# An RWKV layer's work issued in one order written out by hand, in place of a scheduler's order

## The chip, the cores and the metric

The kernel runs on one core of a Trainium2 chip (core 0). The metric is the device time of one execution in microseconds (us). Of the kernel before there are three timed runs, and one further execution was taken by the hardware profiler. The engines are called as in the profile: PE is the matrix engine, PEld its weight loads, DVE the vector engine, ACT the scalar engine, POOL the GpSimd engine, and SP the queue from which all DMA transfers of this kernel are issued.

## The reference, cut to what matters

A stream x of 256 positions by 2048 channels passes an RWKV-7 layer with its MLP, a shared key and value projection, an attention layer with a second MLP, and a last norm. The change touches the first mixing layer only. What it computes:

```python
h = rms_norm(x, mix_norm[0]); prev = h shifted by one position
xs = h + (prev - h) * x_mix                  # six mixes: r, k, v, w, a, g
r, k, v = xs[r] @ w_rkv[0], xs[k] @ w_rkv[1], xs[v] @ w_rkv[2]
decay = exp(-exp(-softplus(-(w0 + tanh(xs[w] @ w1) @ w2)) - 0.5))
a = sigmoid(a0 + (xs[a] @ a1) @ a2);  g = sigmoid(xs[g] @ g1) @ g2
kk = normalised(k * k_k);  k = k * (1 + (a - 1) * k_a)
# per head, S is 64 x 64, frame by frame:
S = S * decay_t + (S @ -kk_t) (kk_t * a_t)^T + v_t k_t^T;   y_t = S @ r_t
y = group_norm(y) * lnx_w + lnx_b + sum(r * k * r_k) * v
x = x + (y * g) @ w_o
```

All weights and all data are float32.

## The kernel before, in words

The 256 positions stand in the free dimension, the 2048 channels in 16 groups of 128 partitions (KT = 16). A weight tile of 512 KB is loaded by `load_split` (L191): SP issues the load to a buffer `wr` (4 buffers), ACT casts it to `wh` (L203), and DVE writes the rest `wl = wr - wh` (L205). Each is a float32r operand, so that a product is made of three matmuls: `wh` by the high part of the data, `wh` by the low part, and `wl` by the high part (`mm3`, L210 to L213). `wh` and `wl` have 5 buffers each.

The layer is cut into streams, each a Python generator that yields between its steps: `h` makes the normalised stream and its differences, `mk`, `mr` and `mv` the mixes for k, r and v, `lw`, `la` and `lg` the small projections of decay, a and gate, `gk`, `gr`, `gv` (four each) the three big projections, `gate` the gate's second product, `prep0` to `prep7` what a unit of four heads needs ahead of its recurrence, `inv0` to `inv7` the inverse of a 64 x 64 triangle per chunk and head, `rec0` to `rec7` the recurrence in four chunks of 64 frames, and `wo0` to `wo3` the first 12 of 16 contraction steps of the output projection. The last four steps of `wo` follow as plain calls of `gemm_group`, and then the MLP begins, whose first matmul is the first that writes a tile `mmw`.

In `rec_steps` (L777) a chunk is a chain: four matmuls of `halves` (L869, tile `zyus`) give zp, DVE copies it to `zt` (L179), eight matmuls follow (L883, L887), ACT copies two halves into `Tt` (L177, "ua" and "ub"), eight more matmuls (L869) give the next state, and DVE adds them to `sw` into the next chunk's `Tt` (L897). POOL has made `sw` from the state before (L182). The inverse is a like chain of 64 x 64 matmuls (L693, tiles i0 to i5), with ACT's copies X and Y (L177) and DVE's product t1 (L731) between. These matmuls use a quarter of the array (tile 64 x 64) or half (128 x 64); those of the projections use all of it (128 x 128).

The order in which all this stands is made twice. `play` (L299) sorts the steps of all streams by the due times in PLAN_A and PLAN_B, and calls them in this order. What the steps issue is then put in order once more, engine by engine, by the scheduler of the language's tile layer, instruction by instruction, from priorities and its own estimate of durations. In part B `share` makes every 10th cast go to DVE (L201) and every 5th subtraction go to POOL (L205).

Of the kernel before, what the change touches and what calls it, by code (L numbers as in the profile page):

```python
# [14 lines left out]
ALU = mybir.AluOpType  # L15
# [38 lines left out]
def shape_constants():  # L54
# [13 lines left out]
    for s in range(6):  # L68
# [5 lines left out]
        if s == 0:  # L74
# [18 lines left out]
SHARE_A = {"h": 0, "l": 0}  # L93
SHARE_B = {"h": 10, "l": 5}
PLAN_A = {
# [6 lines left out]
}  # L102
PLAN_B = {
# [6 lines left out]
}  # L110
AFTER = {"gate": ["lg"], "mv": [f"gk{g}" for g in range(4)], "mr": [],
         "wo2": ["rec5"], "wo3": ["rec5"], "wo0": ["wo2", "wo3"], "wo1": ["wo2", "wo3"]}
AFTER.update({f"prep{u}": [f"gk{u // 2}", "lw", "la"] for u in range(8)})
AFTER.update({f"inv{u}": [f"prep{u}"] for u in range(8)})
AFTER.update({f"rec{u}": [f"inv{u}", "gr0", "gr1", "gr2", "gr3", f"gv{u // 2}", "gate"] for u in range(8)})
# [3 lines left out]
def trunk_kernel(ctx: ExitStack, tc: tile.TileContext, xin, vecs, bfv, c32, c16, w_rkv, w1, w2, a1, a2, g1, g2,  # L119
                 w_o, w_kvf, fox_q, fox_o, w_up, w_down, out):  # L120
    nc = tc.nc
    mm = nc.tensor.matmul
    act = nc.scalar.activation
    V = nc.vector
    G = nc.gpsimd
    dma = nc.sync.dma_start
    ldma = nc.sync.dma_start
    sdma = nc.sync.dma_start
    nc.scalar.preload_act_table_set("natural_log_exp_and_others")

# [44 lines left out]
    def cp(n, o, i):  # L175
        if ENG[n] == "S":
            nc.scalar.copy(o, i)  # L177
        else:
            (V if ENG[n] == "V" else G).tensor_copy(o, i)  # L179
# [11 lines left out]
    share = {"n": 0, "h": 0, "l": 0}  # L191

    def load_split(src, p, nk, n, per=1, wraw=wraw, wsp=wsp):
# [3 lines left out]
        for k in range(0, nk, per):  # L197
            h = wsp.tile([p, per, n], F32R, tag="wh", name="wh")
            c = share["n"] = share["n"] + 1
            if share["h"] and c % share["h"] == 0:  # L200
                V.tensor_copy(h, raw[:, k:k + per, :])  # L201
            else:
                nc.scalar.copy(h, raw[:, k:k + per, :])  # L203
            lo = wsp.tile([p, per, n], F32R, tag="wl", name="wl")
            (G if share["l"] and c % share["l"] == 0 else V).tensor_tensor(  # L205
                lo, raw[:, k:k + per, :], h.bitcast(F32), op=ALU.subtract)
            hl += [(h[:, i, :], lo[:, i, :]) for i in range(per)]
# [73 lines left out]
    def gemm_wide(w, col, x, name, pool, wpools, evac):  # L281

        ps = wide_sums(w, col, x, wpools)
        for b in range(2):
            t = pool.tile([P, 2, T], F32, tag=name, name=name, bufs=3)
            for j in range(2):
                nc.scalar.copy(t[:, j, :], ps[2 * b + j][:, T:2 * T])
# [7 lines left out]
    def play(plan, streams, finished):  # L295

        order = sorted((b + (e - b) * (j + 0.5) / (streams[n][1] + 1), i, n)
                       for i, (n, (b, e)) in enumerate(plan.items()) for j in range(streams[n][1] + 1))
        for _, _, n in order:  # L299
            if n not in finished:  # L300
                assert all(m in finished for m in AFTER.get(n, ())), n
                if next(streams[n][0], finished) is finished:
                    finished.add(n)
        assert all(n in finished for n in plan)
# [61 lines left out]
    def split(src, oh, ol, gp=False):  # L366
        nc.scalar.copy(oh, src)
# [3 lines left out]
    def mlp(layer, norm, pool, wpools, a, b, final):  # L371
# [29 lines left out]
        def finish(g):  # L401

            for j in range(2):
                kp = 2 * g + j
                tp = side("ytp").rearrange("p (k t) -> p k t", k=2)
                for kk in range(2):
                    for i in range(2):
                        n = (2 * kp + kk) * P
                        nc.tensor.transpose(tp[:, kk, i * P:(i + 1) * P], y[:, i, n:n + P], C("ident"))
# [4 lines left out]
        for c in range(FF // D):  # L414
            for g in range(4):
# [10 lines left out]
                if c == 0 and g == 3:  # L426
                    rps = side("rc")
                    for i in range(2):
                        nc.tensor.transpose(rps[:, i * P:(i + 1) * P], r2[:, i * P:(i + 1) * P], C("ident"))
# [53 lines left out]
    G.memset(hT[:, :, 0:1], 0.0)  # L483


# [3 lines left out]
    warm = side("warm")  # L489
    for i in range(12):  # L490
        mm(warm[:, 0:P], ones, ones, start=True, stop=True)
    ps = side("hps")[:, 0:T]
    for i, (k0, k1) in enumerate(XG):
        sq = hT[:, k0:k1, 1:]
        if i % 2 == 0:
            act(sq, xT[:, k0:k1, :], AF.Square)
        else:
            V.tensor_tensor(sq, xT[:, k0:k1, :], xT[:, k0:k1, :], op=ALU.mult)
# [716 lines left out]
```

## Time and profile before

| what | before |
|---|---|
| timed runs | 2467.97, 2468.21 and 2472.01 us; median 2468.21 us |
| the profiled execution, span from first to last instruction | 2470.1 us |
| PE, busy | 2426.3 us, 98% of the span |
| PEld, DVE, ACT, POOL, busy | 2085.5, 1510.2, 1237.9 and 241.2 us |
| first matmul of the MLP (tile mmw) | 641.1 us after the span's start |

The span of the profiled execution is 1.9 us above the median of the runs. A matmul of the profile is pipelined and its end is modelled, so that PE counts as busy from one matmul's start over the next one's: how far PE is from its best shows in the distance from one start to the next, not in its busy share. "PEclk" is the clock that PE was granted. A row of the timeline has the start, the time from the first start to the last end of the instructions merged in it, engine, line, tiles and shapes, and in brackets how long the engine had been idle and what ended that. "issue" means that nothing which the profile shows was waited for.

### The profile page before, as it was taken

What the parts mean: (1) busy time and instruction counts of PE and PEld (TensorE: products, weight loads), DVE (VectorE), ACT (ScalarE), POOL (GpSimd) and SP (SyncE); (2) the same over time, 40 slices, a digit from 0 to 9 for tenths busy, and PEclk for the clock granted to TensorE, in tenths of its full rate; (3) what the DMA queues carried; (4) which work ended last, traced back from release to release, by engine and by line L of the source; (5) the groups of instructions that cost most, each with busy time, mean ns of one, the idle gap of its engine ahead of it and who ended that gap; (6) DMA issues with size and microseconds to landing.
All of it is one profiled execution on the core that took longest, in us unless ns stands there. A gap on an engine that the chain in (4) does not pass through costs nothing.

```text
span 2470.1 us, 45757 instructions
## 1 busy us (share of the span) xinstructions
PE 2426.3 (98%) x18336; PEld 2085.5 (84%) x18336; DVE 1510.2 (61%) x2199; ACT 1237.9 (50%) x1971; POOL 241.2 (10%) x241
## 2 busy tenths in 40 slices
PE   8999999999999999999999999999999999999998
PEld 6899877689888888888888888888888888888886
DVE  8986575665854455554567565777654555555554
ACT  3766454454654453443455544565554543443543
POOL 2000122221310010000011000011010000000001
PEclk9999999999999999999999999999999999999999
DMA  5777765564756666666655656545656666656653
GB/s 165 229 248 247 260 212 174 183 181 154 229 182 196 194 185 194 194 188 192 192 181 178 191 178 195 173 154 178 202 182 196 188 188 195 191 188 196 190 185 125
DMA packets 276565, 472.56 MB, mean 191 GB/s; under 512 B 23280, under 2 KB 70656, under 8 KB 276352
## 3 DMA queue, kind: packets, MB, share of 16 engines
q1 hardware_dynamic: 276352, 469.64, 61.4%
q8 instruction: 143, 2.34, 0.4%
q14 instruction: 70, 0.57, 0.1%
HBM read 445.44 MB, written 24.13 MB: 190 GB/s over the span
## 4 chain that ended last, share of the span: by engine, by line
PE 91%; DVE 4%; issue 2%; DMA 2%; ACT 1%; POOL 0%; SPq 0%; POOLq 0%; DVEq 0%; ACTq 0%
PE mmw L253 21%; PE mmw L257 11%; PE mmd L391 9%; PE mmd L390 9%; PE mmd L389 9%; PE mmn L271 5%; PE mm L211 3%; PE mm L212 3%; PE mm L213 3%; PE mmn L275 2%; PE i L693 1%; PE mmv L767 1%; PE mmv L1047 1%; PE mmv L1046 1%; PE zyus L869 1%
## 5 line engine op out<-in xcount | busy, mean ns | idle before, releaser
L205 DVE TENSOR_TENSOR wl<-wr,wh 128x1024 fp32r<-128x1024 f32 (+1 forms) x1001 | 963.8, 974 | 774.6 <-ACT wh L203 683.5
L203 ACT CAST wh<-wr 128x512 fp32r<-128x512 f32 (+1 forms) x1012 | 841.0, 837 | 976.6 <-PE mmd L390 344.3
L253 PE MATMUL mmw<-opB,wh 128*128 128x512 f32 x1280 | 321.1, 392 | 0.0
L253 PEld LDWEIGHTS mmw<-opB,wh 128*128 128x128 f32 x1280 | 230.3, 189 | 41.8 <-ACT nln L351 0.3
L253 PE MATMUL mmw<-opA,wh 128*128 128x512 f32 x1024 | 256.6, 392 | 0.0
L253 PEld LDWEIGHTS mmw<-opA,wh 128*128 128x128 f32 x1024 | 184.3, 189 | 33.4 <-ACT nln L351 0.3
L389 PE MATMUL mmd<-wh,opA 128*128 128x512 f32 x512 | 199.6, 390 | 0.0
L389 PE MATMUL mmd<-wh,opB 128*128 128x512 f32 x512 | 199.6, 390 | 0.0
L391 PE MATMUL mmd<-wl,opA 128*128 128x512 f32 x512 | 199.2, 389 | 0.0
L390 PE MATMUL mmd<-wh,opB 128*128 128x512 f32 x512 | 199.2, 389 | 0.0
L391 PE MATMUL mmd<-wl,opB 128*128 128x512 f32 x512 | 199.2, 389 | 0.0
L390 PE MATMUL mmd<-wh,opA 128*128 128x512 f32 x512 | 199.2, 389 | 0.0
L419 POOL TENSOR_TENSOR ms<-mt 128x512 f32<-128x512 f32 x64 | 78.6, 1241 | 1158.0 <-ACT mt L417 1158.0
L257 PEld LDWEIGHTS mmw<-opB,wl 128*128 128x128 f32 x1280 | 174.5, 190 | 14.9 <-DVE wl L205 2.6
L257 PE MATMUL mmw<-opB,wl 128*128 128x256 f32 x1280 | 178.7, 282 | 1.8 <-DVE wl L205 1.8
L211 PE MATMUL mm<-opA,wh 128*128 128x256 f32 x512 | 150.5, 294 | 0.0
L257 PEld LDWEIGHTS mmw<-opA,wl 128*128 128x128 f32 x1024 | 139.7, 190 | 10.0
L213 PE MATMUL mm<-opA,wl 128*128 128x256 f32 x512 | 145.2, 284 | 0.8 <-issue 0.8
L212 PE MATMUL mm<-opA,wh 128*128 128x256 f32 x512 | 145.5, 284 | 0.0
L257 PE MATMUL mmw<-opA,wl 128*128 128x256 f32 x1024 | 142.8, 282 | 0.0
L391 PEld LDWEIGHTS mmd<-wl,opA 128*128 128x128 f32 x512 | 96.1, 188 | 20.0
L391 PEld LDWEIGHTS mmd<-wl,opB 128*128 128x128 f32 x512 | 96.1, 188 | 20.0
(293 smaller groups left out, 3818.5 us busy)
## 6 DMA issues: line engine op xcount, KB each, us to landing
wr<-in_mlp_w_up_dram SPq DMA_DIRECT2D x256, 512.0 KB, 3.8
wr<-in_mlp_w_down_dram SPq DMA_DIRECT2D x256, 512.0 KB, 4.0
wr<-in_w_rkv_dram SPq DMA_DIRECT2D x96, 512.0 KB, 4.8
wr<-in_w_kvf_dram SPq DMA_DIRECT2D x64, 512.0 KB, 3.7
wr<-in_w_o_dram SPq DMA_DIRECT2D x32, 512.0 KB, 4.2
wr<-in_fox_w_q_dram SPq DMA_DIRECT2D x32, 512.0 KB, 3.6
wr<-in_fox_w_o_dram SPq DMA_DIRECT2D x32, 512.0 KB, 3.6
wr<-in_g_dram SPq DMA_DIRECT2D x8, 512.0 KB, 4.5
```

The source lines that it names most:

```text
L203: nc.scalar.copy(h, raw[:, k:k + per, :])
L205: (G if share["l"] and c % share["l"] == 0 else V).tensor_tensor(lo, raw[:, k:k + per, :], h.bitcast(F32), op=ALU.subtract)
L211: mm(ps, wh, xh, start=first and bank_first, stop=False, skip_group_check=True)
L212: mm(ps, wh, xl, start=False, stop=False, skip_group_check=True)
L213: mm(ps, wl, xh, start=False, stop=last, skip_group_check=True)
L253: mm(ps[m], h[:, m * P:(m + 1) * P], x[:, k].rearrange("p h t -> p (h t)"), start=k == 0, stop=False, skip_group_check=True)
L257: mm(ps[m][:, 0:T], lo[:, m * P:(m + 1) * P], x[:, k, 0, :], start=False, stop=k == KT - 1, skip_group_check=True)
L271: mm(ps[m], hl[i][0][:, m * P:(m + 1) * P], x[:, k0 + i].rearrange("p h t -> p (h t)"), start=k0 + i == 0, stop=False, skip_group_check=True)
L389: mm(ps[i], b[:, k, 0, t], h, start=k == 0, stop=False)
L390: mm(ps[i], b[:, k, 1, t], h, start=False, stop=False)
L391: mm(ps[i], b[:, k, 0, t], lo, start=False, stop=k == KT - 1)
L419: G.tensor_tensor(s, t, t, op=ALU.mult)
```

## The change: what it does

A thin wrapper stands around each engine (`Tap`): while a `Tape` records, a call is not issued but noted, with the letter of its engine (P for PE, S for ACT, V for DVE, G for POOL, Q for SP) and the step it belongs to. All streams of part A, with the norm at the start as a stream of its own (`first`), are recorded, then those of part B. `record` cuts each stream into pieces: every instruction of ACT, DVE, POOL and SP is a piece, and for PE all matmuls of one step that follow each other. `replay` issues the pieces as two written tables say (2531 pieces, counted in them), and inside `tc.manual_schedule()` this order is the program order of every engine. What follows the layer is put behind its last instruction of each engine (`tc.issue_after`). The due times, `play` and `share` go, so all casts are ACT's and all subtractions DVE's. From the first matmul of the MLP on, the order of all five engines is as before. All instructions of the layer then come from one line (L251) in the changed kernel; L245 is all that is issued outside of the recording.

```diff
-SHARE_A = {"h": 0, "l": 0}
-SHARE_B = {"h": 10, "l": 5}
-PLAN_A = {
-    "mr": (2.914, 3.432), "gk2": (2.618, 3.513), "prep5": (4.992, 5.379), "gk3": (3.79, 4.651),
...
+ORDER_A = """
+firstG firstP lwQ*2 gk0Q firstS gk0Q prep0Q*2 firstP firstV*2 firstS firstP firstG firstV firstP firstV firstP
...
+ORDER_B = """
...
+rec7V wo1V rec7P wo3S wo3V wo1Q wo1S wo3Q*2 rec7S wo1P wo1V rec7S rec7V wo1P wo1S rec7V wo1V rec7S wo1P rec7V wo1S
...
+class Tape:
...
+    def record(self, gen):
+
+        self.ops, self.step = [], 0
+        for _ in gen:
+            self.step += 1
+        ops, self.ops = self.ops, None
+        return ops
...
+        def call(*a, **k):
+            if self._t.ops is None:
+                return f(*a, **k)
+            self._t.ops.append((self._l, self._t.step, f, a, k))
+        return call
...
-            c = share["n"] = share["n"] + 1
-            if share["h"] and c % share["h"] == 0:
-                V.tensor_copy(h, raw[:, k:k + per, :])
-            else:
-                nc.scalar.copy(h, raw[:, k:k + per, :])
+            S.copy(h, raw[:, k:k + per, :])
             lo = wsp.tile([p, per, n], F32R, tag="wl", name="wl")
-            (G if share["l"] and c % share["l"] == 0 else V).tensor_tensor(
-                lo, raw[:, k:k + per, :], h.bitcast(F32), op=ALU.subtract)
+            V.tensor_tensor(lo, raw[:, k:k + per, :], h.bitcast(F32), op=ALU.subtract)
...
+    def record(names):
+        for n in names:
+            last = None
+            for op in tape.record(streams[n]):
+                if op[0] != "P" or op[:2] != last:
+                    rec.setdefault(n + op[0], deque()).append([])
+                rec[n + op[0]][-1].append(op)
+                last = op[:2]
...
+    def replay(order):
+        with tc.manual_schedule():
+            for t in order.split():
+                n, _, c = t.partition("*")
+                for _ in range(int(c or 1)):
+                    for op in rec[n].popleft():
+                        last[op[0]] = emit(n[:-1], op)
...
+        for ins in last.values():
+            behind.enter_context(tc.issue_after(ins.ins))
```

Three places show how instructions move. The first is PE at the very start. Before, behind the norm's matmuls (`hps`), stand those of the first big projection (`mm`, whose data is `opB`):

```order
L491 MATMUL warm<-ones 128x128 x12
L502 MATMUL hps<-hT,ones 128x256 x10
L211 MATMUL mm<-opB,wh 128x256 x2
L212 MATMUL mm<-opB,wh 128x256
L213 MATMUL mm<-opB,wl 128x256
```

In the changed kernel the same place reads:

```order
L251 MATMUL warm<-ones 128x128 x12
L251 MATMUL hps<-hT,ones 128x256 x10
L251 MATMUL lps<-xs,wr 96x256 x8
L251 MATMUL mm<-opB,wh 128x256 x2
L251 MATMUL mm<-opB,wl 128x256
```

Eight matmuls of the decay's small projection (`lps`) have moved ahead of the first big one; they read a mix `xs` as it is, while `opB` is cast and subtracted from it first.

The second place is PE at the third chunk of unit 3 (`zyus_6987` before, `zyus_5315` now; `Tt_6548` and `Tt_5294` are that unit's state). Before, the four matmuls of the chunk's first step and the big ones of `gv` (`mmv`) stand in each other:

```order
L769 MATMUL mmv_7792<-wl_7801,opB_77 128x512
L767 MATMUL mmv_7791<-wh_7855,opB_77 128x512
L869 MATMUL zyus_6987<-Tt_6548,xT_78 64x64
L768 MATMUL mmv_7791<-wh_7855,opB_77 128x512
L869 MATMUL zyus_6987<-Tt_6548,xT_78 64x64 x3
L769 MATMUL mmv_7791<-wl_7857,opB_77 128x512
L767 MATMUL mmv_7792<-wh_7855,opB_77 128x512
L768 MATMUL mmv_7792<-wh_7855,opB_77 128x512
L769 MATMUL mmv_7792<-wl_7857,opB_77 128x512
L883 MATMUL zyus_6987<-Tt_6548,xT_78 64x64 x4
L887 MATMUL zyus_6987<-zt_6986,yf_6547 64x64 x4
```

In the changed kernel the same step reads (i1 is a step of an inverse):

```order
L251 LDWEIGHTS chh_1234
L251 MATMUL i1_1239<-X_1235,chh_1234 64x64
L251 MATMUL mmv_852<-wh_865,opB_77 128x512 x2
L251 MATMUL mmv_852<-wl_866,opB_77 128x512
L251 MATMUL mmv_853<-wh_865,opB_77 128x512 x2
L251 MATMUL mmv_853<-wl_866,opB_77 128x512
L251 MATMUL zyus_5315<-Tt_5294,xT_78 64x64 x4
L251 LDWEIGHTS chh_1187
L251 MATMUL i1_1216<-X_1213,chh_1187 64x64
```

The four matmuls now stand together, behind six big ones and ahead of small ones of an inverse. Counted in the whole order up to the MLP's first matmul, PE goes from one array tile (128 x 128, 128 x 64 or 64 x 64) to another 305 times before and 235 times now.

The third place is POOL in the last units. Before, `sw` of the units 6 and 7 (`Tt_9222`, `Tt_9318`) stands among subtractions `wl`:

```order
L205 TENSOR_TENSOR wl_9448<-wr_9444,wh_9446 128x512
L182 TENSOR_TENSOR k2_9327<-k2_9327,r_9323 128x512
L205 TENSOR_TENSOR wl_9658<-wr_9650,wh_9656 128x512
L182 TENSOR_TENSOR sw_9605<-Tt_9222,WC_111 128x256
L182 TENSOR_TENSOR sw_9701<-Tt_9222,WC_111 128x256
L205 TENSOR_TENSOR wl_9845<-wr_9841,wh_9843 128x512
L182 TENSOR_TENSOR sw_9711<-Tt_9318,WC_111 128x256
L182 TENSOR_TENSOR sw_9874<-Tt_9318,WC_111 128x256
```

Now POOL's queue at the same units (`Tt_5393`, `Tt_5426`) reads:

```order
L251 TENSOR_TENSOR sw_5409<-Tt_5393,WC_111 128x256
L251 TENSOR_TENSOR sw_5412<-Tt_5393,WC_111 128x256
L251 MEMSET Tt_5426 64x128 x2
L251 TENSOR_TENSOR xT_78<-r_5429,e3_5430 128x512
L251 TENSOR_TENSOR xT_78<-k16_87,WC_111 128x512
L251 TENSOR_TENSOR sw_5415<-Tt_5393,WC_111 128x256
L251 TENSOR_TENSOR k2_5431<-k2_5431,r_5429 128x512
L251 TENSOR_TENSOR sw_5442<-Tt_5426,WC_111 128x256
L251 TENSOR_TENSOR sw_5445<-Tt_5426,WC_111 128x256
```

All 23 subtractions of POOL in the layer have gone to DVE, and 12 casts have gone from DVE to ACT.

More of the change, by code (lines that the diff above doesn't have):

```diff
@@ L1 @@
 import math
+from collections import deque
 from contextlib import ExitStack
@@ L92 @@
 }
-SHARE_A = {"h": 0, "l": 0}
-SHARE_B = {"h": 10, "l": 5}
-PLAN_A = {
[6 rows of a table removed]
-}
-PLAN_B = {
[6 rows of a table removed]
[L110 to L115, printed above, removed]
+G4 = range(4)
@@ new lines @@
+STREAMS_A = (["first", "h", "mk"] + [f"gk{g}" for g in G4] + ["la", "lw", "lg", "gate"] + [f"prep{u}" for u in range(8)]
+             + ["mr"] + [f"gr{g}" for g in G4] + ["mv"] + [f"gv{g}" for g in G4] + [f"inv{u}" for u in range(8)])
+STREAMS_B = [f"rec{u}" for u in range(8)] + ["wo2", "wo3", "wo0", "wo1"]
+ORDER_A = """
+firstG firstP lwQ*2 gk0Q firstS gk0Q prep0Q*2 firstP firstV*2 firstS firstP firstG firstV firstP firstV firstP
+firstS*2 hV*2 hG hV*2 hG lwV hV hG lwP lwV hV hG lwP gk0S lwV hG hV gk0S lwP lwV hG hV lwP lwV gk0S hG lwV lwP gk0S
@@ L176, in cp @@
         if ENG[n] == "S":
-            nc.scalar.copy(o, i)
+            S.copy(o, i)
         else:
@@ L293, in gemm_group @@
             pass
[L295 to L304, printed above, removed]
+    def record(names):
[6 more added lines that the diff above has]
+                last = op[:2]
+    last = {}
+    def replay(order):
[5 more added lines that the diff above has]
+                        last[op[0]] = emit(n[:-1], op)
     def merge(*parts):
@@ L963, in after0 @@
         operand("kvn", kp, opBH, opBL)
-    with tc.tile_pool(name="msp0", bufs=WSP, reuse_waits="tile") as ms, \
+    with ExitStack() as behind, tc.tile_pool(name="msp0", bufs=WSP, reuse_waits="tile") as ms, \
             tc.tile_pool(name="mlp0", bufs=2, reuse_waits="tile") as mp:
+        for ins in last.values():
+            behind.enter_context(tc.issue_after(ins.ins))
         for g in range(4):
```

227 lines of the change are left out of this document (175 added, 52 removed), and 11 rows, old and new, of tables (PLAN_A, PLAN_B).

## The prediction

> **What bounds the kernel now.** I read the page, then the busy times by stage, then PE's timeline in the recurrence.
>
> ```profile
> span 2470.1 us, 45757 instructions
> PE 2426.3 (98%) x18336; PEld 2085.5 (84%) x18336; DVE 1510.2 (61%) x2199; ACT 1237.9 (50%) x1971; POOL 241.2 (10%) x241
> ```
>
> PE bounds the whole. The stages, as columns of busy time and count, then granted clock, DMA share and GB/s:
>
> ```profile
> 0.00:120.00 120.00, 107.33 (x697) 94.67 (x698) 104.29 (x209) 70.21 (x146) 14.31 (x25) 0.97 0.63 201
> 120.00:300.00 180.00, 180.00 (x1708) 168.69 (x1707) 131.11 (x236) 112.38 (x217) 8.63 (x8) 1.00 0.76 249
> 300.00:641.00 341.00, 323.62 (x6552) 271.24 (x6551) 221.78 (x409) 159.81 (x328) 80.20 (x86) 0.98 0.60 186
> 641.00:2470.00 1829.00, 1815.33 (x9385) 1550.88 (x9383) 1053.02 (x1347) 895.47 (x1283) 138.08 (x123) 1.00 0.61 186
> ```
>
> The change ends at 641 us; the 1829 us behind it keep their order, and I leave them as they are. A busy share of 95% hides how slow PE goes in the third row, so I go by distances between starts. Back to back, a big matmul of 256 columns takes 0.12 us and an f32 one (`lps`) 6.99 / 32 = 0.218 us (chain of waits):
>
> ```profile
> 600.03 0.12 PE mm L212
> 600.15 0.12 PE mm L213
> 130.65 6.99 PE lps L549 x32
> ```
>
> One of 512 columns takes 0.23 us, and a change of array tile costs more (timeline of PE):
>
> ```profile
> 331.94 0.39 PE L768 MATMUL mmv<-wh,opB 128*128 128x512 f32 x1
> 332.17 0.40 PE L769 MATMUL mmv<-wl,opB 128*128 128x512 f32 x1
> 332.49 0.22 PE L693 MATMUL i<-t,Y 64*64 64x64 f16 x2
> 332.74 0.20 PE L693 MATMUL i<-Y,t 64*64 64x64 f16 x2
> 332.87 0.45 PE L869 MATMUL zyus<-Tt,xT 128*64 128x64 f32 x8
> ```
>
> From 331.94 to 332.17 is 0.23 us; from there to the first 64 x 64 matmul it is 0.32, so 0.09 us go to the change of tile. The 32 small ones up to 332.74 start about 0.01 apart, but the next, of another tile, only 0.13 later: 0.12 lost. I take 0.105 a change.
>
> An estimate of what the first 641 us hold, with counts from the order: 2304 matmuls at 0.12 are 276 us, 384 at 0.23 are 88, 276 f32 ones at 0.218 are 60, and some 5990 others, nearly all of them small at 0.01 to 0.03, about 108; together 532 us of work. The 305 changes of tile are 32 us. That leaves 641 - 564 = 77 us in which PE did nothing. Placed the same way, 22 us of it lie before 120 us (98 us of work there), next to nothing between 120 and 300, and 54 in the recurrence.
>
> **The change part by part.** *Fewer changes of tile.* 305 become 235, because a step's matmuls are one piece: 70 x 0.105 = 7.4 us, all on PE's path. Bounds from the two measured changes: 6.3 to 8.4. I take -7.
>
> *The start.* PE's first big matmul waits 3.93 us for `opB`, at the end of a chain from the norm:
>
> ```profile
> 11.77 1.13 PE L502 MATMUL hps<-hT,ones 128*128 128x256 f32 x4 [0.70 <-DVE hT L500]
> 16.84 0.80 PE L211 MATMUL mm<-opB,wh 128*128 128x256 f32 x2 [3.93 <-ACT opB L367]
> ```
>
> Now eight `lps` (16 records of 0.218, 3.5 us of work) fill this, though the first still waits for its `xs`, some 3 us of the 4. Behind it DVE is short: by the order it has, each instruction at its row's mean, 138 us of work by the time PE has 120 us of its own, and 124 now. Before, DVE was busy 104.29 of 120 us, so PE could not run ahead of it. Counting, for each matmul that waits, the matmul work which stands between it and the matmul its producer needs, the start lacks 17.6 us before and 7.2 now. A part of that stays with DVE: I take -8, with bounds 0 (DVE binds as before) and -14.
>
> *Short hops.* In the recurrence PE waits for results that go through DVE or ACT and back:
>
> ```profile
> 400.17 0.50 PE L769 MATMUL mmv<-wl,opB 128*128 128x512 f32 x1
> 400.48 0.53 ACT L177 COPY Tt<-zyus 64x128 f32<-64x128 f32 x2 [0.74 <-POOL sw L182]
> 401.07 0.69 PE L869 MATMUL zyus<-Tt,L 128*64 128x64 f32 x16 [0.39 <-ACT Tt L177]
> ```
>
> After 400.17, 0.23 of its own and 0.10 for the change, PE was free at 400.50 and began at 401.07. By the same count the recurrence has 48 such places before, 12.6 us in all, and 19 now, 4.6 us. I take -8; bounds: 0, if DVE's queue eats it, and -16, since before more is lost than this count explains.
>
> *POOL's subtractions.* In the row above ACT itself waited for `sw`, which stands in POOL's queue among subtractions of 1.3 us:
>
> ```profile
> L205 POOL TENSOR_TENSOR wl<-wr,wh 128x512 fp32r<-128x512 f32 x21 | 27.8, 1325 | 57.0 <-ACT wh L203 27.6 <-PE mm L213 12.9 <-PE mmv L769 6.0
> L177 ACT COPY Tt<-zyus 64x128 f32<-64x128 f32 x64 | 16.6, 260 | 29.1 <-PE zyus L887 19.8 <-POOL sw L182 4.0 <-PE mm L212 2.2
> L205 DVE TENSOR_TENSOR wl<-wr,wh 128x512 fp32r<-128x512 f32 x85 | 60.9, 721 | 43.1 <-ACT wh L203 31.3 <-PE zyus L887 5.3 <-PE zyus L869 3.8
> L201 DVE CAST wh<-wr 128x512 fp32r<-128x512 f32 x10 | 4.2, 423 | 2.4 <-PE mm L212 1.6 <-PE mmv L768 0.7
> ```
>
> Those 4.0 us of waits go, since no subtraction stands in POOL's queue any more. For it DVE takes 23 x 0.72 = 16.6 us and gives 12 x 0.42 = 5.1 to ACT: 11.5 more on 221.78 of 341 us, beside PE's work. I take -4 for the sum, with bounds -8 and +6 (half of DVE's 11.5 on the path).
>
> *Long stalls and the clock.* Twice PE stops for 2.3 to 2.5 us inside a row of small matmuls, waiting for nothing that the profile shows, and its clock then falls:
>
> ```profile
> 371.93 0.22 PE L807 MATMUL yp<-k,yt 64*64 64x64 f32 x1
> 374.49 0.27 PE L807 MATMUL vp<-db,Tt 64*64 64x64 f32 x1 [2.34 <-issue]
> 468.76 0.45 PE L869 MATMUL zyus<-Tt,L 128*64 128x64 f32 x8 [2.52 <-issue]
> 376.00:390.00 14.00, 13.11 (x327) 10.56 (x326) 8.23 (x15) 5.66 (x13) 2.91 (x3) 0.80 0.63 190
> 390.00:410.00 20.00, 19.15 (x414) 14.38 (x414) 10.74 (x26) 7.16 (x18) 6.36 (x7) 0.91 0.38 110
> 470.00:490.00 20.00, 19.14 (x467) 13.98 (x460) 13.29 (x28) 8.27 (x18) 6.04 (x8) 0.91 0.58 186
> q8 instruction: 1, 0.02, 2.2%
> q8 instruction: 1, 0.02, 1.8%
> ```
>
> The last two rows are of the DMA queues around the two stalls (371.9 to 374.6 and 465.5 to 469 us): one transfer of instructions falls into each. Small matmuls use up instructions fastest. A transfer is 16 KB, 128 matmuls with their loads; in the order, five stretches of 128 hold less than 2.4 us of work before (two to five, by where the cut falls), none to two now. The stalls are 4.9 us, the slower clock 0.20 x 14 + 0.09 x 40 = 6.4. I take -8 of 11; bounds 0 and -11. The Trainium skill ("TensorE: Matmul & The Clock Gate", on the HAM clock gate) has the clock fall after an idle window of about 3.4 us; by it stalls of 2.5 us would cost no clock, and the term would be -5. The rows of 0.80 and 0.91 speak against it here.
>
> *SP's queue.* The transfers are the same 1070. Those of the last contraction steps now stand behind the layer's last stores, which wait for the copies of `wo3`'s sums.
>
> ```profile
> wr<-in_w_o_dram SPq DMA_DIRECT2D x32, 512.0 KB, 4.2
> ```
>
> A load lands 4.2 us after its issue, and behind those stores PE still has nearly all of `wo1`, 12 steps of 12 matmuls, 17 us: I cost this at nothing. With that cover gone it is 4.2 us, once.
>
> Sum: -7 - 8 - 8 - 4 - 8 = -35. From 2470.1 this gives 2435; the profiled execution is 1.9 us over the median of the runs, so 2433.
>
> **The rivals.** *The queues of DVE and ACT take the place (slower).* A chunk goes through DVE twice, `zt` and the sum into `Tt`, 32 + 24 = 56 hops in all, and 32 times through ACT. Both orders are now fixed by hand: if one more subtraction (0.72 us) stands ahead of each hop of DVE and one more cast ahead of each of ACT's,
>
> ```profile
> L203 ACT CAST wh<-wr 128x512 fp32r<-128x512 f32 x95 | 58.6, 619 | 80.8 <-PE mmv L768 42.2 <-PE mm L212 28.0 <-DMA wr<-in_w_rkv_dram 4.0
> ```
>
> 56 x 0.72 + 32 x 0.62 = 40 + 20 = 60 us come back on PE. From 35 of 60 on (58% of the hops) nothing is gained; at three quarters of them, 45, it is -35 + 45 = 10 us slower, 2478. For it: between 320 and 420 us of PE's work the order gives DVE 93 us, and several hops are covered by only 0.5 us of small matmuls. Against: DVE is at 65% in that stage now, and the last units have eight rows of `mm`, 1.44 us, between hops. The Trainium skill ("TensorE: Matmul & The Clock Gate", architectural detail) says that ACT and DVE are strict first in, first out, which is this rival's condition; it holds in both kernels. Chance 0.13.
>
> *Only the tile changes pay.* The waits re-form elsewhere, and the start stays DVE's: -7, 2461. For it: DVE's 104.29 of 120 us. Against: the counts above. Chance 0.12.
>
> *The rest goes too.* My terms leave some 30 us of idle PE in the recurrence which no count explains, waits in queues that a scheduler's wrong durations may have made. If the written order removes half, 15 to 20 us more: 2415. Chance 0.20.
>
> *It doesn't reach the chip.* If both orders met the same DMA limits, no change: 2468. Against: DMA share 0.60 to 0.76. Chance 0.05.
>
> **How the numbers follow.** My forecast, 2433, has 0.50; its own range is 2422 to 2450. About 0.2%, 5 us, is the least that a measurement of this kernel tells from no change. Faster by more: 0.50 + 0.20 + 0.12 = 0.82. Within: 0.05. Slower: 0.13. For the range I leave out the slower rival (0.13) and a tail below 2408 (0.05), which would need all unexplained idle time gone as well; so 2408 to 2468.
>
> **What would show it.** Right: the MLP's first matmul at about 606 us in place of 641; PE's granted clock 1.00 through the recurrence; no stall of over 2 us; ACT's `Tt` without a wait for POOL; about 0.09 to 0.12 us still lost at each change of tile. Wrong: that first matmul no earlier than 634 us, DVE busy over 85% of the recurrence, and `zyus` waiting on `zt` and `Tt` behind a `wl`. If instead the part behind 641 us is not 1829 us long, my leaving it alone was wrong.

## The result and the profile after

The changed kernel takes 2447.5 us (median of 4 runs, 2444.1 to 2448.9) beside 2469.6 us of the kernel before on the same chip: 0.9906 of it, 95% interval 0.9891 to 0.9920, 22 us. The forecast was 2433, with a range of 2408 to 2468. The direction and the range held, the narrower range of 2422 to 2450 too; the gain is a little under two thirds of the one forecast, and one term of the sum gave nothing.

The two profiled executions differ by 2470.1 - 2444.9 = 25.2 us. First the page of the changed kernel (share of busy time and count by engine), then its stages; the columns are those of the table by stage in the prediction:

```profile
span 2444.9 us, 45691 instructions
PE 2407.0 (98%) x18336; PEld 2077.2 (85%) x18336; DVE 1520.3 (62%) x2210; ACT 1246.9 (51%) x1983; POOL 217.0 (9%) x218
```

```profile
0.00:120.00 120.00, 111.72 (x765) 99.88 (x766) 100.73 (x200) 66.94 (x132) 14.46 (x25) 0.96 0.62 201
120.00:300.00 180.00, 179.00 (x2126) 165.87 (x2125) 139.72 (x258) 123.50 (x238) 0.40 (x2) 1.00 0.71 240
300.00:616.00 316.00, 300.55 (x6065) 259.91 (x6064) 228.17 (x409) 161.75 (x334) 61.71 (x69) 0.98 0.66 206
616.00:2444.00 1828.00, 1815.72 (x9388) 1551.50 (x9386) 1051.64 (x1346) 894.67 (x1282) 140.48 (x123) 1.00 0.60 186
```

The part behind the layer is 1828 us long, as before, so that the whole gain lies in the layer. Its end is the first matmul of the MLP; the rows of that tile have the first start behind the three durations, before and after:

```profile
L253 PE MATMUL mmw<-opB,wh x1280: 388/389/582, 641.4 to 1447.0; 128*128 128x512 f32 x183
```

```profile
L245 PE MATMUL mmw<-opB,wh x1280: 387/390/582, 616.7 to 1421.4; 128*128 128x512 f32 x183
```

That is 24.7 us earlier. Where they come from can be counted as in the prediction: each matmul at its price by distance between starts, 0.105 us for each change of tile, and what is left is time in which PE did nothing (all matmuls of the trace priced one by one come to 542 us of work, in place of the 532 that the prediction had from the order's counts):

| first start of the MLP | work | changes of tile | idle up to 190 us | idle behind it |
|---|---|---|---|---|
| before, 641.1 us | 542.4 | 305, 32.0 us | 22.1 | 44.6 |
| after, 616.5 us | 542.4 | 235, 24.7 us | 16.0 | 33.4 |

(The starts here are counted from a zero some 0.2 us later than that of the rows above. With other prices for the small matmuls, their mean distances up to 0.12 us, work is 526.2 in both and the idle time is higher by the same amount; its two differences become 6.3 and 11.0.) So the changes of tile gave 7.3 us, the start 6.1, and the idle time of the recurrence 11.2.

In the start the waits show what went. Before, and then after, between 12 and 120 us; the columns are total, times and longest:

```profile
PE mm L211 <- ACT opB L367: 5.4, 4, 3.9
PE kss L599 <- ACT hsh L177: 3.2, 3, 1.5
```

```profile
PE lps L251 <- DVE xs L251: 4.8, 3, 4.2
PE mm L251 <- DVE opB L251: 0.2, 1, 0.2
```

The first wait is no shorter: it only has another matmul at its end (`lps` for `xs`, 4.2 us). What went are three waits of `kss`, the sums over a head, for ACT, which in the written order stand far enough behind what makes them.

In the recurrence the table of waits was to lose its long stalls. Its rows with "issue", time in which PE waits for nothing that the profile shows, before and after:

```profile
PE zyus L869 <- issue: 2.5, 1, 2.5
PE vp L807 <- issue: 2.3, 1, 2.3
PE btb L807 <- issue: 1.3, 1, 1.3
PE mm L213 <- issue: 0.8, 1, 0.8
PE bs L807 <- issue: 0.7, 1, 0.7
PE mmv L769 <- issue: 0.7, 1, 0.7
PE zyus L883 <- issue: 0.4, 1, 0.4
PE i L693 <- issue: 0.3, 1, 0.3
```

```profile
PE i L251 <- issue: 3.4, 2, 2.9
PE g2a L251 <- issue: 1.8, 1, 1.8
PE bs L251 <- issue: 1.7, 2, 1.1
PE btb L251 <- issue: 1.5, 2, 1.2
PE vp L251 <- issue: 0.7, 1, 0.7
PE bta L251 <- issue: 0.5, 1, 0.5
```

Together 9.0 us before and 9.6 after: they moved to other matmuls. The clock is as low as before too (the changed kernel; the granted clock is the third column from the end):

```profile
338.00:345.00 7.00, 4.64 (x94) 3.56 (x95) 1.59 (x4) 2.65 (x5) 0.00 (x0) 0.76 1.06 289
400.00:410.00 10.00, 9.37 (x161) 7.81 (x159) 2.84 (x8) 2.62 (x6) 0.31 (x1) 0.66 0.63 196
540.00:546.00 6.00, 5.91 (x79) 5.39 (x80) 1.94 (x4) 1.54 (x5) 0.00 (x0) 0.72 0.28 91
```

0.24 x 7 + 0.34 x 10 + 0.28 x 6 = 6.8 us of clock lost, where the prediction counted 6.4 before. In the trace's record of the clock the recurrence has 13.7 us at half speed in both kernels.

The two longest of these stalls after the change show what they are. The timeline of PE around the first (start, duration, and in brackets the idle time ahead of it):

```profile
337.26 0.20 PE L251 MATMUL i<-Y,t 64*64 64x64 f16 x2
340.36 0.26 PE L251 MATMUL i<-t,Y 64*64 64x64 f16 x2 [2.90 <-issue]
```

The DMA queues (packets, MB, share of the engines) from 333.2 us to the stall, and then in the stall:

```profile
q1 hardware_dynamic: 794, 1.46, 103.9%
```

```profile
q1 hardware_dynamic: 548, 1.00, 102.5%
q8 instruction: 1, 0.02, 2.6%
```

The one transfer of instructions falls into the stall, with every DMA engine full of data. Counting PE's matmuls, weight loads and semaphore instructions from the start of the trace, 16 of the 27 gaps of over 0.6 us from one start to the next behind 190 us, in both kernels together, stand at one remainder, instruction 192 or 193 of a block of 256 (the others have a row that names an engine, or none): there a new block begins. A block's transfer mostly starts while PE works on the block ahead of it (up to 1.9 us earlier between 190 us and the MLP). Three blocks of the changed kernel; the first and the last row go from about the block's start to about the start of the transfer for the next one, the middle row over the whole block (the last columns are clock, DMA share and GB/s):

```profile
333.20:337.60 4.40, 4.00 (x127) 3.31 (x128) 2.27 (x5) 2.31 (x4) 0.57 (x1) 1.00 1.04 333
434.70:439.80 5.10, 5.10 (x116) 3.85 (x110) 4.75 (x11) 3.48 (x8) 0.00 (x0) 1.00 0.44 100
439.90:443.50 3.60, 3.59 (x124) 2.83 (x124) 3.52 (x8) 1.81 (x4) 2.30 (x5) 1.00 1.00 285
```

In the middle one the transfer starts 0.3 us behind the block's start and nothing is lost at 440.1 us, where the next block begins. In the first and the last, DMA engines full, it starts 4.4 and 3.7 us behind it, takes 1.1 and 1.3 us, and PE goes on 1.4 us after that: stalls of 3.1 and 2.0 us between starts. So a stall is the delay of the transfer, its duration and these 1.4 us, less the time that PE needs for the block: for the first, 4.4 + 1.1 + 1.4 - 3.8 = 3.1.

Blocks that PE gets through in under 3.5 us did become fewer, 7 before and 4 after, as the prediction said of the order. The new stalls of over 1 us came in blocks of 3.8 to 4.6 us, behind transfers that started 3.4 to 4.4 us late. The two stalls that the prediction read in the kernel before are of the same kind: the blocks take PE 2.6 and 3.7 us, and the transfers start 2.9 and 4.0 us behind their starts. A short block alone costs less there: one of 3.3 us at 514 us, whose transfer starts after 0.9 us, loses nothing, and one of 2.4 us at 326 us, whose transfer starts after 0.8 us and takes 1.9, loses 1.6. What fills the DMA engines need not be weights: between 333.4 and 340.4 us SP issues a unit's own data (`k`, `b`, `r`, `e`, `xT`, `Tt`), behind four weight tiles issued from 327 to 332 us.

The Trainium skill ("Runtime: NRT & Kernel Launch", instruction fetch mechanics) has the instructions come in blocks of 256, and the crossing into a block mostly hidden. The repeated remainder bears out the first. By count the second holds too, since 9 of some 60 blocks of the changed kernel behind 190 us begin with a gap of over 0.6 us; but its waits for nothing come to 9.6 us in one layer.

### The profile page after: what moved, and what is told of

Same layout as the page of the kernel before. It is cut to its first block, busy times and chain, and to the rows that moved or that the text cites. A ratio compares the mean times of both kernels' runs of the same rounds, so it can differ in the third digit from the quotient of the medians.

```text
span 2444.9 us, 45691 instructions
## 1 busy us (share of the span) xinstructions
PE 2407.0 (98%) x18336; PEld 2077.2 (85%) x18336; DVE 1520.3 (62%) x2210; ACT 1246.9 (51%) x1983; POOL 217.0 (9%) x218
## 4 chain that ended last, share of the span: by engine, by line
PE 92%; DVE 4%; issue 2%; DMA 1%; ACT 0%; POOL 0%; SPq 0%; POOLq 0%; DVEq 0%; ACTq 0%
PE mmw L245 32%; PE mmd L245 28%; PE mm L251 9%; PE mmn L245 7%; PE mmv L251 4%; PE mmv L245 4%; PE zyus L251 2%; PE i L251 1%; DVE wl L251 1%; PE lps L251 1%; PE mm L245 1%; DVE xs L251 1%; PE lo L251 1%; PE mmg L251 1%; DVE wl L245 0%
## 5 line engine op out<-in xcount | busy, mean ns | idle before, releaser
L245 DVE TENSOR_TENSOR wl<-wr,wh 128x1024 fp32r<-128x1024 f32 (+1 forms) x784 | 810.0, 1044 | 698.4 <-ACT wh L245 623.1
L245 ACT CAST wh<-wr 128x1024 fp32r<-128x1024 f32 (+1 forms) x784 | 702.6, 901 | 833.2 <-PE mmd L245 344.3
L245 PE MATMUL mmw<-opB,wh 128*128 128x512 f32 x1280 | 321.2, 393 | 0.2 <-ACT wh L245 0.2
L245 PE MATMUL mmd<-wh,opA 128*128 128x512 f32 x1024 | 315.8, 390 | 0.0
L245 PE MATMUL mmd<-wh,opB 128*128 128x512 f32 x1024 | 315.8, 390 | 0.0
L245 PEld LDWEIGHTS mmw<-opB,wh 128*128 128x128 f32 x1280 | 230.3, 189 | 42.2 <-ACT wh L245 0.4
L245 PE MATMUL mmw<-opA,wh 128*128 128x512 f32 x1024 | 256.7, 392 | 0.0
L245 PEld LDWEIGHTS mmd<-wh,opA 128*128 128x128 f32 x1024 | 191.7, 188 | 39.5
L245 PEld LDWEIGHTS mmd<-wh,opB 128*128 128x128 f32 x1024 | 191.7, 188 | 39.5
L245 PEld LDWEIGHTS mmw<-opA,wh 128*128 128x128 f32 x1024 | 184.4, 189 | 33.3 <-ACT nln L245 0.3
L251 ACT CAST wh<-wr 128x512 fp32r<-128x512 f32 x240 | 144.9, 617 | 116.4 <-PE mm L251 50.1
L245 PE MATMUL mmd<-wl,opA 128*128 128x512 f32 x512 | 199.3, 389 | 0.0
L245 PE MATMUL mmd<-wl,opB 128*128 128x512 f32 x512 | 199.2, 389 | 0.0
L251 DVE TENSOR_TENSOR wl<-wr,wh 128x512 fp32r<-128x512 f32 x240 | 169.3, 719 | 38.3 <-ACT wh L251 32.1
L245 PEld LDWEIGHTS mmw<-opB,wl 128*128 128x128 f32 x1280 | 174.5, 190 | 13.5 <-DVE wl L245 1.0
L245 POOL TENSOR_TENSOR ms<-mt 128x512 f32<-128x512 f32 x64 | 78.5, 1239 | 1158.8 <-ACT mt L245 1158.8
L245 PE MATMUL mmw<-opB,wl 128*128 128x256 f32 x1280 | 178.6, 282 | 0.6 <-DVE wl L245 0.6
L251 PE MATMUL mm<-opA,wh 128*128 128x256 f32 x896 | 171.4, 291 | 0.2 <-DVE opA L251 0.2
L245 PEld LDWEIGHTS mmw<-opA,wl 128*128 128x128 f32 x1024 | 139.7, 190 | 10.0
L251 PEld LDWEIGHTS mm<-opA,wh 128*128 128x128 f32 x896 | 141.7, 192 | 3.8 <-DVE opA L251 0.4
L245 PE MATMUL mmw<-opA,wl 128*128 128x256 f32 x1024 | 142.8, 282 | 0.0
L251 PE MATMUL mm<-opA,wl 128*128 128x256 f32 x448 | 127.2, 284 | 0.0
```

Of the source, the lines that this page charges most:

```text
L245: return f(*a, **k)
L251: return op[2](*op[3], **op[4])
```

## The experiments

All runs are against the kernel before on the same chip, in five rounds each: it took 2474.4 us beside the first four rows of the table, 2471.4 beside the next four and 2473.8 beside the last four. The times in the texts put on record ahead of the runs are on the scale of the first comparison (2469.6), so the ratio is what compares with them. The last column is of one profiled execution each. The theory: the gain is the order's, through fewer changes of tile, waits in the start, and short waits in the recurrence; the stalls stay, since blocks of instructions come late behind loads. The rivals: it was POOL's share, or that nothing is moved by a scheduler any more; and the stalls are a matter of small matmuls alone.

| run | us | ratio to before, 95% interval | MLP's first matmul, us |
|---|---|---|---|
| before without the shares | 2478.1 | 1.0024 (1.0014 to 1.0034) | 644.6 |
| changed, shares put back | 2446.5 | 0.9890 (0.9874 to 0.9905) | 616.9 |
| first table alone | 2474.1 | 1.0001 (0.9990 to 1.0012) | 646.2 |
| both tables, scheduler on | 2455.6 | 0.9929 (0.9917 to 0.9941) | 624.2 |
| changed, no loads of gv, wo | 2431.0 | 0.9833 (0.9819 to 0.9846) | 601.1 |
| changed, 40 steps cut | 2455.3 | 0.9934 (0.9921 to 0.9946) | 623.5 |
| changed, blocks moved | 2452.3 | 0.9920 (0.9907 to 0.9934) | 619.3 |
| changed, lps behind | 2450.9 | 0.9918 (0.9905 to 0.9932) | 618.2 |
| changed, again | 2446.3 | 0.9898 (0.9880 to 0.9915) | 627.0 |
| changed, 64 filling | 2442.9 | 0.9870 (0.9853 to 0.9886) | 615.1 |
| changed, 80 filling | 2443.4 | 0.9875 (0.9861 to 0.9889) | 614.8 |
| before, no loads of gv, wo | 2458.0 | 0.9938 (0.9926 to 0.9950) | 630.2 |

**The shares, alone.** One line of the kernel before:

```diff
-SHARE_B = {"h": 10, "l": 5}
+SHARE_B = {"h": 0, "l": 0}
```

> The kernel before, with POOL's share of the subtractions and DVE's share of the casts taken out and nothing else. Theory (the written order carries the gain, the shares are worth a few us): 0 to 6 us under before, 2464 to 2470 us. Rival (POOL's subtractions were what the recurrence lost): at least 10 us under before, 2460 us or less.

It is slower, by 6 us as the ratio has it and by 3.7 between the medians (the MLP begins 3.2 us later), so both were wrong: taking POOL's subtractions away costs the kernel before something. ACT's copies `Tt` wait for `sw` as before, 5.5 us here and 4.0 there, with no subtraction in POOL's queue:

```profile
L177 ACT COPY Tt<-zyus 64x128 f32<-64x128 f32 x64 | 16.6, 260 | 26.9 <-PE zyus L887 16.5 <-POOL sw L182 5.5 <-PE mm L212 2.2
```

**The shares put back into the written order.** They take the same places in the table (condensed):

```diff
+            c = shared["n"] = shared["n"] + shared["on"]      # on: recording gv, wo
-            S.copy(h, raw[:, k:k + per, :])
+            (VS.tensor_copy if c and shared["on"] and c % 10 == 0 else S.copy)(h, raw[:, k:k + per, :])
-            V.tensor_tensor(lo, ...)
+            (GV if c and shared["on"] and c % 5 == 0 else V).tensor_tensor(lo, ...)
```

> The changed kernel, with both shares put back for the loads of gv and wo (every fifth subtraction on POOL, every tenth cast on DVE) at the same places of the written order. Theory: 0 to 6 us over the changed kernel, 2447 to 2454 us, with waits of ACT for sw of POOL in the recurrence again. Rival: the 11 us that the recurrence's waits became shorter come back, 2458 us or more.

Nothing comes back: the MLP begins at 616.9 us, beside 616.7. POOL has 22 subtractions of 1.34 us again, and `Tt` does not wait for `sw`:

```profile
L251 POOL TENSOR_TENSOR wl<-wr,wh 128x512 fp32r<-128x512 f32 x22 | 29.4, 1337 | 344.1 <-PE mmv L251 196.5 <-ACT wh L251 79.7 <-PE mm L251 32.8
```

```profile
L251 ACT COPY Tt<-zyus 64x128 f32<-64x128 f32 x64 | 16.7, 260 | 16.3 <-PE zyus L251 13.7 <-POOL xT L251 1.1 <-PE i L251 0.5
```

The wait for `sw` went by where `sw` stands, not by who subtracts. The time is within the interval of the changed kernel's, at the lower end of what the theory had or a little under it; the theory's wait of ACT for `sw` did not come.

**The first table alone.** What the table leaves of each stream is handed over by the old due times, to the scheduler:

```diff
-    replay(ORDER_B)
+    play(PLAN_B)      # per stream, per step: the recorded instructions not yet issued
```

> The first table alone: projections and their neighbours in the written order, the recurrence by the planner's times and the scheduler, without the shares. Theory (6 to 7 us of the gain come from the start, the rest from the recurrence): PE is about 6 us ahead of before at 120 us and gains nothing more after that, 2458 to 2466 us, with about 300 tile changes. Rival (the start is no part of it): 2468 us or more. Second rival (the recurrence gains from what has been issued ahead of it, not from its own order): 2450 us or less.

The time, a ratio of 1.0001, is in the range of the first rival, but not for its reason. By stage the first half of the theory holds: PE has 104.6 us of its work done at 120 us and 279.5 at 300 (97.9 and 273.3 before). But all of it is lost again in the recurrence, which has 27 us at half clock and 56 us of idle time behind 190 us. The due times were made for another state of the streams, and the shares are out too, so how much of this is the order's own cannot be read from this run. That the recurrence would gain from what was issued ahead is not borne out, with the same reservation.

**Both tables, but the scheduler may move what they hand over.**

```diff
-        with tc.manual_schedule():
+        with ExitStack():
```

> The same two tables, but handed to the scheduler, which may move instructions as its own durations say (242 tile changes in place of 235). Theory (what counts is the order in which the pieces are handed over): 2447 to 2457 us. Rival (what counts is that nothing is moved any more): 2460 us or more.

The ratio of 0.9929 is 2452 us on the first comparison's scale, as the theory had it. Some 70 to 75% of the gain come with the order in which pieces are handed over, the rest with its being kept. (The record of the clock has 20.5 us at half speed in this layer in place of 13.7, so that up to 3.4 us of the rest may be the clock's.) One place where it is lost: PE waits 2.6 us at 205 us for DVE's `chh`,

```profile
PE i L251 <- DVE chh L251: 2.6, 1, 2.6
```

where the changed kernel waits 0.5.

**The changed kernel without the loads of gv and wo.** Casts and subtractions read a constant (condensed):

```diff
+        if bare["on"]:                      # recording gv, wo
+            raw = k32[:, 0:512]             # in place of a loaded tile
+        else:
             raw = wraw.tile([p, nk, n], F32, tag="wr", name="wr")
             dma(raw, src)
```

> The changed kernel without the weight loads of gv and wo: their casts and subtractions read a constant that lies in SBUF, everything else stays. (It leaves out these loads, so the values of these products are not the reference's.) Theory (the fetches of PE's instructions are late because they wait behind weight loads): in the recurrence PE's waits for nothing that the profile shows go from 9.6 us to under 3 us, none over 1 us, and the granted clock is 1.00 throughout; 2434 to 2441 us. Rival (small matmuls use up instructions faster than a fetch takes, whatever the loads do): 8 to 10 us of such waits and some 14 us at half clock remain, 2444 to 2450 us.

The MLP begins 15.6 us earlier. The stage from 300 us to there, and all its rows of "issue" there:

```profile
300.00:601.00 301.00, 293.87 (x6076) 255.96 (x6075) 227.00 (x409) 162.68 (x336) 61.85 (x68) 1.00 0.44 135
```

```profile
PE zyus L251 <- issue: 1.2, 1, 1.2
PE mmv L251 <- issue: 1.1, 1, 1.1
PE bs L251 <- issue: 0.8, 1, 0.8
```

3.1 us in place of 9.6, the clock at 1.00, so these loads are what makes most blocks late. Not all of it: three stalls of about 1 us stay. One is behind a block of 2.4 us whose transfer started after 0.6 us, and here the rival has its part; the other two are behind blocks of 4.3 and 3.4 us whose transfers started 3.0 and 2.4 us late, at a DMA share of 0.60 and 0.93 without these loads. The time is 3 us under the theory's range as measured here, and 6 on the first comparison's scale (2428); waits that name an engine became shorter by some 2 us as well, and the rest is not traced.

**Forty steps cut in two.** Condensed, in `replay`: behind the first half of a step of `rec` or `inv`, where a piece of big matmuls comes next, one of these is issued first:

```diff
+                if held and n[-1] == "P":
+                    ops, held = ops[:1] + held + ops[1:], []
+                elif n[:3] in ("rec", "inv") and n[-1] == "P" and len(ops) > 3 and big_piece_next(names, i):
+                    ops, held = ops[:len(ops) // 2], ops[len(ops) // 2:]
```

> The changed kernel with 40 steps of the recurrence and the inverses cut in two around a big matmul: 315 tile changes in place of 235, the same matmuls. Theory (a change costs 0.105 us on PE's path): 80 x 0.105 = 8.4 us over the changed kernel, 2454 to 2458 us. Rival (the changes fall into time in which PE waits for a result anyway): less than 3 us over it, 2447 to 2450 us.

The MLP begins 6.8 us later, for 80 changes: 0.085 us each on the path. The ratio, 0.9934 beside 0.9906 and 0.9898, says 7 to 9 us. The price of a change holds, and with it the term of 7 us (70 changes are 6.0 us at this run's price).

**The blocks moved.** More filling matmuls at the start:

```diff
         for i in range(12):
             mm(warm[:, 0:P], ones, ones, start=True, stop=True)
+        for i in range(32):
+            mm(warm[:, 0:1], ones, ones[:, 0:1], start=True, stop=True)
```

> The changed kernel with 32 matmuls of one column more behind the warming ones, in the time in which PE waits for the input: 64 matmul records, so every place at which a new block of 256 instructions begins lies 64 records earlier in the recurrence. Theory (a fetch ends at a fixed place of each block and is late by chance of the loads): the waits for nothing sit at other matmuls, again at one remainder of the instruction number by 256, and come to 6 to 13 us; 2443 to 2452 us. Rival (they belong to the matmuls at which they stand): the same matmuls, the same 9.6 us.

Two things, in opposite directions. The filling is not free: a record of a one-column matmul (each matmul is two) takes as long as one of 128 columns, 0.11 and at half clock 0.21 us, so that PE reaches `hps` at 16.7 us and not at 5.9 and the start is 10 us longer:

```profile
4.79 12.04 PE L251 MATMUL warm<-ones 128*128 128x128 f32 x71
16.70 1.63 PE L251 MATMUL hps<-hT,ones 128*128 128x256 f32 x3
```

Behind 190 us PE is idle for 26.2 us in place of 33.4: the rows of "issue" come to 6.4 us in place of 9.6, and the record of the clock has 6.8 us at half speed in place of 13.7. The longest stalls stand at remainder 192 or 193 again, at other matmuls:

```profile
453.90 0.24 PE L251 MATMUL i<-X,chh 64*64 64x64 f16 x3 [3.56 <-issue]
```

That is the theory; the rival is refuted.

**The decay's matmuls among the first big ones.** Tokens of the first table:

```diff
-... lwV hV hG lwP lwV hV hG lwP gk0S ... lwP gk0P mkV gk0Q ...
+... hV hG hV hG gk0S ... gk0P mkV lwV gk0Q hV lwP gk0Q ...      # eight lwV and lwP, one of each in four tokens
```

> The changed kernel, with the first eight mixes and matmuls of the decay's projection moved from ahead of the first big matmuls to among them. Theory (they fill PE while the first operand is made): 1 to 4 us over the changed kernel, 2448 to 2452 us, all of it before 60 us. Rival (the time there is set by DVE, whatever PE has first): within 1 us of the changed kernel.

PE waits 7.7 us for `opB` in place of 4.2 for `xs`,

```profile
PE mm L251 <- ACT opB L251: 7.7, 1, 7.7
```

and has 2.8 us less of its work done at 120 us (101.6). That is within the theory's 1 to 4 us. The MLP begins 1.5 us later, and by the runs alone (0.9918) the intervals overlap.

**Three runs together with the changed kernel itself.** This last was to be a measure only.

> The changed kernel itself, unchanged, as the measure for the three runs beside it: 0.990 to 0.992 of before, the profile as at first.

Its ratio is the first one's. But its six runs go from 2444.8 to 2457.8, and the profiled execution is the longest, with the same instructions in the same order: the MLP begins at 627.0 us, not 616.7. From 300 us on:

```profile
300.00:627.00 327.00, 306.90 (x6070) 265.53 (x6069) 228.66 (x409) 161.72 (x334) 62.01 (x68) 0.95 0.65 199
```

```profile
PE i L251 <- issue: 4.5, 3, 2.2
PE bs L251 <- issue: 3.3, 2, 2.2
PE btb L251 <- issue: 2.6, 1, 2.6
PE mmv L251 <- issue: 2.3, 1, 2.3
...
PE g2a L251 <- issue: 1.1, 1, 1.1
```

With two smaller rows (0.8 and 0.4) 15 us of such waits in place of 9.6, and 30.7 us at half clock in place of 13.7, make the difference. The places are block beginnings again, some with longer and some with shorter stalls than before. So what a late block costs differs from one execution to the next by some 10 us, and a single profile of this stage says that little about small effects.

**Filling that costs nothing, 64 and 80 matmuls.**

```diff
+        half = ones[0:64, :].bitcast(F16)
+        for i in range(64):      # and 80
+            mm(warm[0:64, 0:64], half[:, 0:64], half[:, 64:128], start=True, stop=True)
```

> The changed kernel with 64 matmuls of 64 x 64 in half precision behind the warming ones: the blocks of instructions begin at the same matmuls as in the run with the moved cut, but the filling takes 1 to 2 us of a wait and not 10 us of the path. Theory (where a block begins decides what a late fetch costs; the moved cut lost 26.2 us in place of 33.4 behind 190 us): 4 to 8 us under the changed kernel, the waits at the matmuls of that run. Rival (it depends on the moment at which loads happen to come, and the 7 us were chance): within 3 us of the changed kernel, and the waits at other matmuls than in that run.

> The same with 80 filling matmuls. Reckoned over the blocks of the recurrence, the time by which blocks are shorter than 4.5 us comes to 4.1 us, against 5.1 without filling and 7.2 with 64. Theory (short blocks decide): the smallest sum of waits of the three, 3 to 9 us under the changed kernel. Rival (which loads are under way decides): no smaller than with 64.

With 64, the block's beginning that lost 3.56 us in the run with the moved blocks is again the worst place, at the same matmul:

```profile
448.41 0.31 PE L251 MATMUL i<-X,chh 64*64 64x64 f16 x3 [4.38 <-issue]
```

It is the same instruction of the trace, and the block ahead of it takes PE 2.9 us in both, with transfers that start 3.9 and 4.7 us behind its start. So the place is set by where blocks begin; that the size goes by which loads are under way is likely, not shown. The rows of "issue" come to 8.9 us with 64 and 8.5 with 80. The times are 3.4 and 2.8 us under the changed kernel's median in this comparison, with intervals that overlap its own; all eight of these runs are below its six. That these two are a little faster than the changed kernel is likely, not settled. The reckoning by short blocks, which had 80 before 64, was not borne out: they can't be told apart.

**The kernel before without the same loads.** The same edit as above, in its `load_split` (condensed):

```diff
+        if bare:                            # gv, wo
+            raw = k32[:, 0:512]
```

> The kernel before, without the weight loads of gv and wo, as was done with the changed one. (Their values are not the reference's.) Theory (the loads hold up the fetches and results of both orders alike, so that they hide nothing of the change): 12 to 20 us under before, and the changed kernel without them stays some 20 to 28 us under this one. Rival (the written order only moved the loads' price about): under 8 us below before, or the difference between the two without loads is 30 us or more, the 35 us that had been forecast.

It gains 15 us (0.9938), the changed kernel 17 (0.9833 beside the mean of 0.9906 and 0.9898, x 2472). Its rows of "issue" come to 2.4 us in place of 9.0, and its recurrence has 3.4 us at half clock in place of 13.7, so in this order too the loads make most of both. Without these loads the change is worth 0.9938 - 0.9833, 26 us, with some 4 us either way by the two intervals: within the theory's 20 to 28, though the rival's 30 is not excluded. The profiles have 630.2 - 601.1 = 29.1 us, of which 2.8 are waits in this run for a unit's own data, `k` and `b`, that arrive late:

```profile
PE g2a L811 <- DMA k<-s_k: 2.1, 1, 2.1
PE g2a L811 <- DMA b<-s_b: 0.7, 1, 0.7
```

So the loads hide a few us of the change at most, and not 10.

## Why the prediction was right, and which term was not

- **Nothing behind 641 us.** Right: 1829 us before, 1828 after.
- **Changes of tile, -7.** Right: 70 fewer, 7.3 us at the prediction's price, and 80 more cost 6.8.
- **The start, -8 with bounds 0 and -14.** Right in size, 6.1 us. Of its two reasons, the eight `lps` alone are worth 2.8 (run with them behind). The first wait did not shrink, as the text had said of most of it. The rest is where waits of `kss` went; that DVE's queue had bound them was argued and not tried.
- **Short hops, -8, and POOL's subtractions, -4.** Together right, 11.2 us of idle time behind 190 us, of which no part is stalls or clock. The split was wrong, and that the sum of the two came out so near is luck as far as POOL's part goes: the shares give nothing in the written order, and taking them from the scheduler's costs 4 to 6 us. ACT's wait for `sw` did go, but by its place in the order. By these runs the 11.2 belong to the order of the pieces; which hops they are is not resolved further, since most of it is in gaps of under 0.25 us.
- **Long stalls and half clock, -8 of 11.** This step failed. The prediction put the stalls down to blocks with too little work, counted that these became fewer, and let the stalls and the slow clock go with them. The count was right, 7 short blocks and then 4, but the stalls are 9.0 and then 9.6 us, and the clock loss is 6.8 by the record in both. Nor is that one execution's chance: of the seven other profiles of the written order with its loads and no scheduler none has under 6.4 us of stalls. Shortness is only one part of a stall; the other, which the prediction put at nothing, is how late the transfer starts, and it is late where loads fill the DMA engines: DMA share 1.04 and 1.00 in the first and the last of the block rows above, where the prediction's rows of 0.60 to 0.76 had hidden it in means. Taking the loads of `gv` and `wo` away took 6.5 of 9.6 us of stalls and all of the slow clock, and in the kernel before 6.6 of 9.0. This term is 8 of the 10 us between the 35 forecast and the 24.7 that the profile shows, the start 2 more; the 22 us of the runs are within what one profile differs from another.
- **SP's queue, 0.** Nothing shows against it.
- **The rivals.** The slower one did not come about: DVE is busy for 228.17 of 316 us, 72%, and PE's waits for `Tt` come to 1.7 us. "Only the tile changes pay" is refuted by the start and the idle time; "the rest goes too" by the 33 us of idle time that are left; "it doesn't reach the chip" by the 22 us.
- **The signs.** The MLP's first matmul at 616.7 us lies between the 606 and the 634 that were named. The clock at 1.00 and no stall of over 2 us did not come: 0.98, and a stall of 2.9.

## What to carry to other kernels

A wait that the profile puts down to nothing, at equal distances of 256 instructions on one engine, can be code that came late, as here; ask what else the DMA engines were doing in the microseconds ahead of it, not only how small the instructions are. Price an edit's parts one by one, and where a term rests on a cause that was only counted, ask for a second condition that must hold with it. An order that is kept by hand makes room for changes (who subtracts, here) that cost something when a scheduler moves the rest around them.

## What the runs showed of the hardware

- A block of PE's instructions, 256 of them, starts to be fetched, where blocks are short, mostly 0.2 to 1.5 us behind the start of the block ahead when DMA is at half load or less, and 1 to 4.4 us behind it when it is full; behind all four stalls of over 1 us in the changed kernel it was 3.4 us or more. Taken in order, one transfer to a block, no block begins less than 1.27 us behind its transfer's end in either kernel; after a stall PE goes on 1.3 to 1.6 us behind it.
- PE's clock falls to half for multiples of 3.41 us (3.4, 6.8 and 10.2 in the record). In the changed kernel it fell at 401.4 us behind two stalls of 0.7 and 0.8 us, and not at 446 us behind one of 2.0. By the rule of the Trainium skill that the prediction cited ("TensorE: Matmul & The Clock Gate", the HAM clock gate) stalls of 2.5 us should cost no clock. No length of a stall alone decides it here.
- A float32 matmul of one column takes as long as one of 128, 0.11 us for each of its two records at full clock.
